# Squares of the MLP norms taken tile by tile behind the projections, and the decode step traced later, in a two-layer hybrid decoder step

## The chip, the core and the metric

The kernel runs on one core of a Trainium2 chip. The core has a matrix engine (PE in the profile), a vector engine (DVE), a scalar engine (ACT), a general engine (POOL), a queue engine that mostly issues DMAs (SP), and sixteen DMA engines. Each engine takes its instructions in the order in which they stand in its own queue, and waits there for what the next one needs. The metric is the device time of one execution in microseconds (us). Of the kernel before there are three timed runs, and one execution with a profile.

## The reference

One step of a decoder with two layers over 1,040 prompt positions (16 learned ones ahead of 1,024) and 8 decode tokens, with model width 1024 and MLP width 4096, all in fp32:

```python
for i in range(DEPTH):                       # layer 0: Conformer convolution; layer 1: RWKV-7
    hn = rmsnorm(h, norm_mix[i])
    out = conformer_conv(hn, ...) if i == 0 else rwkv7(hn, ...)
    h = h + out                              # out ends in a 1024x1024 projection (w_pw2, w_o)
    m = rmsnorm(h, norm_mlp[i])
    h = h + square(relu(m @ w_mlp_in[i])) @ w_mlp_out[i]
y = rmsnorm(h, norm_final)
# rmsnorm(x, g) = x * rsqrt(mean(x * x) + eps) * g
```

The decode tokens go through the same layers. In RWKV-7 each has a state of its own, 16 heads of 64x64, which is updated once (`S = S*w + sa*(kk*a) + v*k`, `y = S*r`); this is the "decode step" below. The prompt's RWKV-7 part runs in chunks of 64 positions.

## The kernel before

Activations lie transposed: 128 features on the partitions, eight tiles (k or m = 0 to 7) for the width of 1024, and up to 352 positions along the free axis. The positions are cut in three groups, g = 0, 1, 2. Every product is exact to fp32 by a split in a high and a low part: for each 128x128 block of weights PE does three matmuls (`mm3`, L187 to L189). ACT makes the high part of each weight (L157) and POOL subtracts to get the low part (L162, in pieces of 256 columns); activations are split by ACT (`hh`, `m_h`, `z_h`) and DVE (`hl`, `m_l`, `z_l`).

Layer 0 runs `post(0)`, `post(1)`, `post(2)` one after the other, about 300 us each. Each does the projection `pw2` (eight `ps_o` products, each added to `h` by DVE at L562), the norm of the MLP (`mlp_in`), and then the MLP: for j = 0 to 31 a product `ps_in` (24 matmuls), on which DVE applies relu and the norm's factor (`r`, L306), ACT squares (`s`) and splits; two steps later the products `out`, added to `h` by DVE at L319. Beside the MLP other work is handed out by `filler` at its points: the norm `norm_out(g-1)` of the group before, which makes the input of layer 1, the convolution of the next group and its layer norm. Behind `post(2)` comes `norm_out(2)` and the RWKV part. Layer 1 then runs `mixer_out(0)` (the projection `ps_oo` out of RWKV, added to `h` by DVE at L1459), the MLP of group 0, `mixer_out(1)`, `mixer_out(2)`, the MLP of groups 1 and 2 together, and the final norm. The recurrence of the last chunks (`until`), the decode step and the norms of the RWKV output (`norm_gates`, transposes on PE and work of DVE on `ey`, `eq`, `ez`) are handed out along `mixer_out(0)` and that first MLP.

A mean of squares in the kernel before is taken in one go, behind the last tile of `h`: ACT squares the eight tiles (L218), POOL adds the even ones up in one accumulator and DVE the odd ones in another (L223), and PE multiplies both by a constant matrix (`st_m`, `st_d`, L231), which sums over the partitions and spreads the mean over all of them. ACT takes the root, DVE the reciprocal (`rs`, L238). In `mlp_in` this stands behind the loop that makes `m_h` and `m_l` (L246, L247); the factor `rs` is used only at L306. In `norm_out` the factor is multiplied into `h` (L575).

The order on each engine is not the order of the code: a scheduler simulates the engines with a cost model and sets each queue's order from that, and the calls of `filler` set when a piece of side work becomes available to it.

## Time and profile before

| | us |
|---|---|
| median of three runs | 2909.58 (2907.05 to 2913.22) |
| profiled execution | 2902.45 |
| its span, first to last instruction | 2900.7 |
| PE busy in the span | 2682.1 (92%) |
| DVE, POOL, ACT busy | 1972.2 (68%), 1709.3 (59%), 1345.9 (46%) |
| mean granted clock of PE | 0.955 of full speed |

The profiled execution lies 7.1 us below the median of the runs, and 1.75 us of it lie outside the span. In the rows below, "[4.98 <-DVE h L319]" behind an instruction says that its engine had been idle for 4.98 us before it, and that the last thing it waited for was DVE's instruction on line 319 that writes `h`. Matmuls overlap, so their durations are longer than the distance from one to the next.

### The profile page before, as it was taken

The page shows a single profiled execution, that of the slowest core. Times are in us where ns is not written, and L with a number is a line of the kernel's source. Part 1 is how long each engine was busy: PE and PEld are TensorE (multiplying, and loading weights), DVE is VectorE, ACT ScalarE, POOL GpSimd, SP SyncE. Part 2 cuts the span into 40 slices and gives each one's busy share as a digit, 9 for nine tenths or more (in the row PEclk, how much of TensorE's full clock was granted, in tenths as well). Part 3 has the DMA queues.
Part 4 walks back from the last instruction along what each step waited for, and adds up shares of the span by engine and source line. Part 5 has one row for each costly group of instructions (what it writes and reads, how often), then busy time and mean ns, then how long its engine had stood idle before and what let it go on. Part 6 is the DMA issues. An engine that isn't in the chain of part 4 may idle for free.

```text
span 2900.7 us, 54435 instructions
## 1 busy us (share of the span) xinstructions
PE 2682.1 (92%) x20522; PEld 2561.1 (88%) x20522; DVE 1972.2 (68%) x3807; ACT 1345.9 (46%) x2511; POOL 1709.3 (59%) x2298
## 2 busy tenths in 40 slices
PE   8999899999998998877899889969999989999998
PEld 7999899989997998867788688858889989999998
DVE  5999999994476446367978786679856654443444
ACT  5545444543454334464666665634355542222223
POOL 6677778877787775445434453565548773433432
PEclk9999999999999999888899899989999999999999
DMA  6663444454445442676787787685567642222211
GB/s 180 171 184 93 139 133 138 144 157 138 139 145 164 139 139 86 197 196 168 212 206 207 204 214 181 174 209 152 134 169 224 183 135 85 66 69 70 66 59 41
DMA packets 659285, 428.34 MB, mean 148 GB/s; under 512 B 126840, under 2 KB 609208, under 8 KB 659022
## 3 DMA queue, kind: packets, MB, share of 16 engines
q1 hardware_dynamic: 652780, 421.93, 51.8%
q10 hardware_dynamic: 6018, 2.89, 0.4%
q8 instruction: 162, 2.65, 0.4%
q14 instruction: 101, 0.83, 0.1%
q0 software_dynamic: 224, 0.03, 0.0%
HBM read 353.03 MB, written 72.66 MB: 147 GB/s over the span
## 4 chain that ended last, share of the span: by engine, by line
PE 34%; DVE 6%; POOL 4%; DMA 3%; issue 2%; ACT 2%; SPq 0%; DVEq 0%; ACTq 0%; POOLq 0%
PE out L187 3%; PE ps_in L187 3%; PE ps_in L188 3%; PE out L188 3%; PE ps_in L189 3%; PE out L189 3%; POOL wo_lo L162 2%; PE A L1178 2%; POOL wi_lo L162 2%; DVE tt L1137 1%; PE ps_oo L187 1%; PE ps_oo L188 1%; PE ps_oo L189 1%; PE p_k L188 1%; PE p_k L187 1%
## 5 line engine op out<-in xcount | busy, mean ns | idle before, releaser
L162 POOL TENSOR_TENSOR wo_lo<-wo_raw,wo_hi 128x256 fp32r<-128x256 f32 x736 | 557.2, 789 | 309.7 <-ACT wo_hi L157 274.9
L162 POOL TENSOR_TENSOR wi_lo<-wi_raw,wi_hi 128x256 fp32r<-128x256 f32 x640 | 493.2, 802 | 274.3 <-ACT wi_hi L157 272.7
L187 PE MATMUL out<-hh,wo_hi 128*128 128x352 f32 (+2 forms) x1536 | 504.8, 329 | 31.2 <-ACT hh L140 15.5
L319 DVE TENSOR_TENSOR h<-h,out 128x352 f32<-128x352 f32 (+2 forms) x768 | 385.7, 510 | 194.2 <-PE out L189 193.6
L187 PE MATMUL ps_in<-m_h,wi_hi 128*128 128x352 f32 (+2 forms) x1536 | 497.8, 324 | 11.1 <-ACT m_h L246 10.5
L188 PE MATMUL out<-hh,wo_lo 128*128 128x352 f32 (+2 forms) x1536 | 498.9, 325 | 0.0
L189 PE MATMUL ps_in<-m_l,wi_hi 128*128 128x352 f32 (+2 forms) x1536 | 495.4, 323 | 2.7 <-DVE m_l L247 2.7
L188 PE MATMUL ps_in<-m_h,wi_lo 128*128 128x352 f32 (+2 forms) x1536 | 497.0, 324 | 0.0
L189 PE MATMUL out<-hl,wo_hi 128*128 128x352 f32 (+2 forms) x1536 | 491.9, 324 | 2.9 <-DVE hl L141 2.9
L483 DVE SCALAR_TENSOR_TENSOR cv<-u,wdw,cv 128x352 f32<-128x352 f32 (+2 forms) x720 | 378.0, 576 | 0.8
L157 ACT CAST wi_hi<-wi_raw 128x1024 fp32r<-128x1024 f32 x160 | 168.0, 1050 | 406.1 <-PE out L189 205.0
L157 ACT CAST wo_hi<-wo_raw 128x1024 fp32r<-128x1024 f32 x184 | 192.8, 1049 | 331.8 <-PE out L189 152.4
L187 PEld LDWEIGHTS out<-hh,wo_hi 128*128 128x128 f32 x1536 | 293.6, 191 | 39.7 <-DVE h L319 18.9
L187 PEld LDWEIGHTS ps_in<-m_h,wi_hi 128*128 128x128 f32 x1536 | 291.0, 189 | 13.2 <-ACT m_h L246 10.6
L189 PEld LDWEIGHTS out<-hl,wo_hi 128*128 128x128 f32 x1536 | 290.3, 190 | 4.8 <-DVE hl L141 4.3
L188 PEld LDWEIGHTS out<-hh,wo_lo 128*128 128x128 f32 x1536 | 293.4, 191 | 1.3
L189 PEld LDWEIGHTS ps_in<-m_l,wi_hi 128*128 128x128 f32 x1536 | 290.0, 189 | 4.6 <-DVE m_l L247 3.6
L188 PEld LDWEIGHTS ps_in<-m_h,wi_lo 128*128 128x128 f32 x1536 | 290.4, 189 | 1.6 <-issue 0.3
L306 DVE SCALAR_TENSOR_TENSOR r<-ps_in,rs_m 128x352 f32<-128x352 f32 (+2 forms) x192 | 98.5, 516 | 240.4 <-PE ps_in L189 233.2
L141 DVE TENSOR_TENSOR hl<-s,hh 128x352 fp32r<-128x352 f32 (+2 forms) x192 | 138.5, 723 | 102.6 <-ACT hh L140 102.4
L308 ACT ACTIVATE s<-r 128x352 f32<-128x352 f32 (+2 forms) x192 | 93.4, 490 | 134.8 <-DVE r L306 132.5
L1178 PE MATMUL A<-xa,bk 128*128 128x256 f32 x272 | 79.7, 412 | 16.9 <-DMA bk<-d_ab 12.2
(388 smaller groups left out, 6197.8 us busy)
## 6 DMA issues: line engine op xcount, KB each, us to landing
wi_raw<-in_w_mlp_in_dram SPq DMA_DIRECT2D x160, 512.0 KB, 4.1
wo_raw<-in_w_mlp_out_dram SPq DMA_DIRECT2D x160, 512.0 KB, 3.8
wr_raw<-in_rwkv_w_r_dram SPq DMA_DIRECT2D x32, 512.0 KB, 4.6
wk_raw<-in_rwkv_w_k_dram SPq DMA_DIRECT2D x32, 512.0 KB, 4.4
wv_raw<-in_rwkv_w_v_dram SPq DMA_DIRECT2D x32, 512.0 KB, 5.7
d_ab<-ab SPq DMA_DIRECT2D x32, 512.0 KB, 5.1
pg_raw<-in_conv_w_pw_dram SPq DMA_DIRECT2D x24, 512.0 KB, 4.9
pa_raw<-in_conv_w_pw_dram SPq DMA_DIRECT2D x24, 512.0 KB, 5.6
```

The costliest lines, as they stand in the source:

```text
L141: eng_lo.tensor_sub(lo, src, hi.bitcast(F32))
L157: nc.scalar.copy(hi[:, :a * b], raw[:, :a * b])
L162: eng_lo.tensor_sub(lo[:, cs], raw[:, cs], hi[:, cs].bitcast(F32))
L187: nc.tensor.matmul(ps, w[0], act[0], start=first, stop=False)
L188: nc.tensor.matmul(ps, w[1], act[0], start=False, stop=False)
L189: nc.tensor.matmul(ps, w[0], act[1], start=False, stop=last)
L306: nc.vector.scalar_tensor_tensor(r[:, :n], ps[:, :n], 0.0, rs[:, :n], op0=ALU.max, op1=ALU.mult)
L308: nc.scalar.activation(s[:, :n], r[:, :n], AF.Square)
L319: nc.vector.tensor_add(hv[:, 4 * i + m, :], hv[:, 4 * i + m, :], ps[:, :n])
L483: nc.vector.scalar_tensor_tensor(acc[m][:, :n], ug[:, m, j:j + n], wdw[:, m, j:j + 1], acc[m][:, :n], op0=ALU.mult, op1=ALU.add)
L1137: nc.vector.tensor_mul(o, ni[:, :j, j:j + 1].broadcast_to([B, j, wd]), ni[:, j:j + 1, j + 1:].broadcast_to([B, j, wd]))
L1178: nc.tensor.matmul(ps[:, i * 2 * P:(i + 1) * 2 * P], bk[:, j + i, :], xa[:, j + i].rearrange("p q x -> p (q x)"), start=True, stop=True)
```

## The change

The squares of a norm are now issued one by one, each behind the instruction that finishes its tile of `h`. `square_sums` gives a function `add(k, src)`, which squares tile k on ACT; the first tiles of each engine are held, the middle ones are added by the engines in turn, and the last two squares go to PE as they are. A mean so has up to four matmul inputs instead of two (accumulators and the squares of tiles 6 and 7). For the MLP norms POOL and DVE take turns; for `norm_out(0)` and `norm_out(1)` POOL alone adds, with three inputs for PE. In layer 0 the squares lie in `u[g]`, the convolution's input, which nobody reads any more by then (for `norm_out(2)` in temporary tiles); in layer 1 in three temporary buffers of their own (`sq`). The mean and `rs` of an MLP norm are now traced ahead of the loop for `m_h` and `m_l`. In layer 1 the side stream changes its order: the norms of the RWKV output of group 1 come first, then the decode step.

```diff
             for i, acc in enumerate(accs):
-                nc.tensor.matmul(ps[:, :n], ones_d, acc[:, :n], start=i == 0, stop=i == 1)
+                nc.tensor.matmul(ps[:, :n], ones_d, acc[:, :n], start=i == 0, stop=i == len(accs) - 1)
             return ps
+        def square_sums(n, name, place, engs, tag="acc"):
+            out, first = [], []
+            def add(k, src):
+                sq = place(k)
+                nc.scalar.activation(sq, src, AF.Square)
+                i = k % len(engs)
+                if k >= KT - 2:
+                    out.append(sq)
+                elif k < len(engs):
+                    first.append(sq)
+                else:
+                    if k < 2 * len(engs):
+                        out.append(stat(f"acc_{name}{i}", f"{tag}{i}", 1))
+                        a, b = out[i][:, :n], first[i]
+                    else:
+                        a = b = out[i][:, :n]
+                    engs[i].tensor_add(a, b, sq)
+            return add, out
...
-        def mlp_in(pl, hv, n, layer, name):
+        def mlp_in(pl, hv, n, layer, name, sums):
+            rs = rstd_of(mean_bcast(sums, n, name), n, 0, name, "rsm", 2)
             ah, al = new_act(pl, name, cur["wide"])
...
-            with tc.high_priority(offset=HP):
-                rs = rstd_of(mean_bcast(mean_parts(hv, n, name, True), n, name), n, 0, name, "rsm", 2)
             return ah, al, rs
...
-            def pw2(g, act):
+            def pw2(g, act, add):
...
                     nc.vector.scalar_tensor_tensor(h[g][:, m, :n], ps[:, :n], vec("b_pw2", m), h[g][:, m, :n],
                                                    op0=ALU.add, op1=ALU.add)
+                    add(m, h[g][:, m, :n])
...
             def norm_out(g):
...
-                parts = mean_parts(hv, n, f"d{g}", True)
-                yield MW
+                if g < 2:
+                    add, parts = square_sums(n, f"d{g}", lambda k: u[g][:, k, :n], (nc.gpsimd,), "accd")
+                else:
+                    add, parts = square_sums(n, f"d{g}", lambda k: tt(f"sqd{k}", "t1")[:, :n], (nc.gpsimd, nc.vector), "accm")
+                for k in range(KT):
+                    add(k, hv[:, k, :])
+                    yield MW / KT
...
-                pw2(g, ln_act[g])
+                add, sums = square_sums(n, f"m0{g}", lambda k: u[g][:, k, :n], (nc.gpsimd, nc.vector), "accm")
+                pw2(g, ln_act[g], add)
...
-            def mixer_out(g, residp, actp, fill):
+            def mixer_out(g, residp, actp, fill, add):
...
                     nc.vector.tensor_add(h1[:, m, :n], h1[:, m, :n], ps[:, :n])
+                    add(m, h1[:, m, :n])
...
+            def sums_of(g):
+                n = G2[g][1]
+                return square_sums(n, f"m1{g}", lambda k: cur["tmp"].tile([P, cur["n"]], F32, name=f"sq{g}_{k}", tag="sq", bufs=3)[:, :n],
+                                   (nc.gpsimd, nc.vector))
...
-                                ([decode_step(), norm_gates(GN_OF[1]), ng2], NGA))
-            mixer_out(0, residp, actp, fill)
+                                ([norm_gates(GN_OF[1]), decode_step(), ng2], NGA))
+            add, sums = sums_of(0)
+            mixer_out(0, residp, actp, fill, add)
```

Lines shift by 21 to 28 in the changed file: L306 becomes L327, L319 L340, L562 L583, L1459 L1487.

DVE where `post(2)` passes from its projection into its MLP, before: `ps_o2_7` is the last product of the projection, `acc_m02` belongs to the MLP's norm, `acc_d1` to `norm_out(1)`.

```order
L223 TENSOR_TENSOR acc_m021_9770<-acc_m021_9770,sq_m023_9772 128x348
L223 TENSOR_TENSOR acc_m021_9770<-acc_m021_9770,sq_m025_9775 128x348
L562 SCALAR_TENSOR_TENSOR h0_2_9459<-ps_o2_7_9715,pvec_85,h0_2_9459 128x348
L247 SCALAR_TENSOR_TENSOR m02_l_9742<-h0_2_9459,pvec_85,m02_h_9741 128x348
L223 TENSOR_TENSOR acc_m021_9770<-acc_m021_9770,sq_m027_9778 128x348
L238 RECIPROCAL rs_m02_9786<-sd_m02_9784 128x348
L223 TENSOR_TENSOR acc_d11_9824<-acc_d11_9824,sq_d13_9826 128x348
L223 TENSOR_TENSOR acc_d11_9824<-acc_d11_9824,sq_d15_9829 128x348
L223 TENSOR_TENSOR acc_d11_9824<-acc_d11_9824,sq_d17_9832 128x348
L306 SCALAR_TENSOR_TENSOR r0_0_2_9847<-ps_in0_0_2_9799,rs_m02_9786 128x348
```

The same place after the change:

```order
L583 SCALAR_TENSOR_TENSOR h0_2_9440<-ps_o2_5_9636,pvec_85,h0_2_9440 128x348
L270 SCALAR_TENSOR_TENSOR m02_l_9746<-h0_2_9440,pvec_85,m02_h_9745 128x348
L253 TENSOR_TENSOR acc_m021_9588<-acc_m021_9588,u2_125 128x348
L270 SCALAR_TENSOR_TENSOR m02_l_9746<-h0_2_9440,pvec_85,m02_h_9745 128x348
L583 SCALAR_TENSOR_TENSOR h0_2_9440<-ps_o2_6_9673,pvec_85,h0_2_9440 128x348
L270 SCALAR_TENSOR_TENSOR m02_l_9746<-h0_2_9440,pvec_85,m02_h_9745 128x348
L583 SCALAR_TENSOR_TENSOR h0_2_9440<-ps_o2_7_9709,pvec_85,h0_2_9440 128x348
L270 SCALAR_TENSOR_TENSOR m02_l_9746<-h0_2_9440,pvec_85,m02_h_9745 128x348
L260 RECIPROCAL rs_m02_9743<-sd_m02_9741 128x348
L327 SCALAR_TENSOR_TENSOR r0_0_2_9801<-ps_in0_0_2_9774,rs_m02_9743 128x348
L327 SCALAR_TENSOR_TENSOR r0_1_2_9841<-ps_in0_1_2_9816,rs_m02_9743 128x348
```

The three adds of `acc_d1` are gone from between `rs_m02` and the first `r`; those of `acc_m02` stand between the adds of the projection.

DVE at the end of `mixer_out(0)` before, from its last product but one to its last (`Sdec`, `t4`, `sa` belong to the decode step, `tt13`, `ni13` to the inverse for a chunk):

```order
L1358 TENSOR_REDUCE sa_23283<-t43_23737 128x4
L1359 TENSOR_TENSOR Sdec3_23736<-Sdec3_23736,dq_23071 128x256
L1137 TENSOR_TENSOR tt13_12_24174<-ni13_23884 128x228
L1360 TENSOR_TENSOR t43_23737<-sa_23283,dq_23071 128x256
L223 TENSOR_TENSOR acc_m101_23340<-acc_m101_23340,sq_m103_23342 128x328
L1138 TENSOR_TENSOR ni13_23884<-ni13_23884,tt13_12_24174 128x12x19
L1361 TENSOR_TENSOR Sdec3_23736<-Sdec3_23736,t43_23737 128x256
L1137 TENSOR_TENSOR tt13_11_24198<-ni13_23884 128x220
L1362 TENSOR_TENSOR t43_23737<-dq_23071 128x256
L223 TENSOR_TENSOR acc_m101_23340<-acc_m101_23340,sq_m105_23345 128x328
L1138 TENSOR_TENSOR ni13_23884<-ni13_23884,tt13_11_24198 128x11x20
L1459 TENSOR_TENSOR h1_0_22622<-h1_0_22622,ps_oo0_7_23270 128x328
```

After the change, around the same two adds (`sv`, `xa`, `nr` belong to the recurrence, `ey`, `ems` to the norms of the RWKV output):

```order
L1213 TENSOR_TENSOR xa1_12572<-A116_23171,m_ar_12477 64x2x64
L1214 TENSOR_TENSOR nr11_22923<-A116_23171,m_ar_12477 128x2x64
L1487 TENSOR_TENSOR h1_0_22592<-h1_0_22592,ps_oo0_6_23197 128x328
L1487 TENSOR_TENSOR h1_0_22592<-h1_0_22592,ps_oo0_7_23287 128x328
L270 SCALAR_TENSOR_TENSOR m10_l_23330<-h1_0_22592,pvec_85,m10_h_23329 128x328 x6
L1410 TENSOR_REDUCE ems4_0_23467<-ey4_0_23315 128x8
L270 SCALAR_TENSOR_TENSOR m10_l_23330<-h1_0_22592,pvec_85,m10_h_23329 128x328
L1411 SCALAR_TENSOR_TENSOR ey4_0_23315<-ems4_0_23467,ey4_0_23315 128x512
```

The decode step has left this stretch, and the adds of the squares have moved up ahead of it.

DVE in the MLP of group 0 of layer 1, from the factor of step j = 8 on, before:

```order
L306 SCALAR_TENSOR_TENSOR r1_8_0_24864<-ps_in1_8_0_24799,rs_m10_23356 128x328
L1364 TENSOR_TENSOR t414_24893<-Sdec14_24892,dq_23071 128x256
L1365 TENSOR_REDUCE yd_23284<-t414_24893 128x4
L1357 TENSOR_TENSOR t415_25013<-Sdec15_25012,dq_23071 128x256
L141 TENSOR_TENSOR hl10_8_24798<-s1_8_0_24866,hh10_8_24797 128x328
L1358 TENSOR_REDUCE sa_23283<-t415_25013 128x4
L1287 TENSOR_TENSOR fs13_24751<-S13_24697,wc_12552 128x512
L1359 TENSOR_TENSOR Sdec15_25012<-Sdec15_25012,dq_23071 128x256
L1360 TENSOR_TENSOR t415_25013<-sa_23283,dq_23071 128x256
L1185 TENSOR_TENSOR xa0_12601<-A144_24755,m_ar_12507 64x2x64
L1186 TENSOR_TENSOR nr14_24570<-A144_24755,m_ar_12507 128x2x64
```

The same place after:

```order
L327 SCALAR_TENSOR_TENSOR r1_8_0_24818<-ps_in1_8_0_24753,rs_m10_23327 128x328
L1385 TENSOR_TENSOR t40_24958<-Sdec0_24957,dq_24824 128x256
L141 TENSOR_TENSOR hl10_8_24752<-s1_8_0_24820,hh10_8_24751 128x328
L1386 TENSOR_REDUCE sa_24955<-t40_24958 128x4
L1387 TENSOR_TENSOR Sdec0_24957<-Sdec0_24957,dq_24824 128x256
L1315 TENSOR_TENSOR fs13_24712<-S13_24658,wc_12522 128x512
L1388 TENSOR_TENSOR t40_24958<-sa_24955,dq_24824 128x256
L1213 TENSOR_TENSOR xa0_12571<-A144_24716,m_ar_12477 64x2x64
L1214 TENSOR_TENSOR nr14_24545<-A144_24716,m_ar_12477 128x2x64
L1389 TENSOR_TENSOR Sdec0_24957<-Sdec0_24957,t40_24958 128x256
L1213 TENSOR_TENSOR xa0_12571<-A144_24716,m_ar_12477 64x2x64
```

Before, the decode step is in its last pieces (`Sdec14`, `Sdec15`) here; after, it begins (`Sdec0`), and 134 of its 144 DVE instructions stand between the steps j = 8 and j = 15, where the 30 instructions of the gates that stood there are gone.

## Rows read from the trace of the kernel before

**Rows 1.** Page, part 1: engine busy us (share of the span) xinstructions.
```profile
PE 2682.1 (92%) x20522; PEld 2561.1 (88%) x20522; DVE 1972.2 (68%) x3807; ACT 1345.9 (46%) x2511; POOL 1709.3 (59%) x2298
```

**Rows 2.** PE timeline: start, us, instruction [idle before it <-releaser]; seven longest related waits.
```profile
608.88 0.66 PE L187 MATMUL out<-hh,wo_hi 128*128 128x348 f32 x1 [4.98 <-DVE h L319]
...
901.92 0.66 PE L187 MATMUL out<-hh,wo_hi 128*128 128x348 f32 x1 [13.13 <-ACT hh L140]
...
1162.67 0.59 PE L187 MATMUL p_g<-hxh,g_hi 128*128 128x272 f32 x1 [8.15 <-ACT hxh L140]
...
1959.07 0.64 PE L187 MATMUL ps_in<-m_h,wi_hi 128*128 128x328 f32 x1 [10.46 <-ACT m_h L246]
...
2339.80 0.86 PE L231 MATMUL st_m<-acc_m,ones_d 128*128 128x352 f32 x2 [1.95 <-POOL acc_m L223]
2343.33 0.66 PE L187 MATMUL ps_oo<-z_h,wo_hi 128*128 128x352 f32 x1 [2.67 <-ACT z_h L140]
...
2384.40 0.43 PE L189 MATMUL ps_in<-m_l,wi_hi 128*128 128x352 f32 x1 [2.43 <-DVE m_l L247]
```

**Rows 3.** Same view, DVE, in the wait that ends at 901.9.
```profile
890.74 7.02 DVE L223 TENSOR_TENSOR acc_d<-acc_d,sq_d 128x348 f32<-128x348 f32 x1 [3.17 <-ACT sq_d L218]
898.31 0.52 DVE L223 TENSOR_TENSOR acc_d<-acc_d,sq_d 128x348 f32<-128x348 f32 x1 [0.56 <-ACT sq_d L218]
899.39 0.52 DVE L223 TENSOR_TENSOR acc_d<-acc_d,sq_d 128x348 f32<-128x348 f32 x1 [0.56 <-ACT sq_d L218]
```

**Rows 4.** Same view, POOL, in the same wait.
```profile
890.14 2.76 POOL L162 TENSOR_TENSOR wi_lo<-wi_raw,wi_hi 128x256 fp32r<-128x256 f32 x4
...
893.74 2.75 POOL L162 TENSOR_TENSOR wo_lo<-wo_raw,wo_hi 128x256 fp32r<-128x256 f32 x4
896.47 0.91 POOL L223 TENSOR_TENSOR acc_d<-acc_d,sq_d 128x348 f32<-128x348 f32 x1
```

**Rows 5.** Windows: stretch, length, busy (instructions) by engine, PE clock, DMA share, GB/s.
```profile
902.00:905.50 3.50, 3.50 (x13) 3.50 (x14) 1.86 (x5) 1.78 (x5) 0.00 (x0) 0.52 0.00 0
```

**Rows 6.** DVE timeline at the second group of the layer-1 MLP.
```profile
2375.84 7.54 DVE L223 TENSOR_TENSOR acc_m<-acc_m,sq_m 128x352 f32<-128x352 f32 x2 [1.48 <-ACT sq_m L218]
```

**Rows 7.** DVE timeline ahead of the wait that ends at 1162.67.
```profile
1154.09 5.22 DVE L575 SCALAR_TENSOR_TENSOR h<-h,pvec,rs_d 128x348 f32<-128x348 f32 x8
```

**Rows 8.** DVE timeline in the wait that ends at 1959.07.
```profile
1955.42 1.05 DVE L1359 TENSOR_TENSOR Sdec<-Sdec,dq 128x256 f32<-128x256 f32 x1
...
1957.23 0.41 DVE L1360 TENSOR_TENSOR t<-sa,dq 128x256 f32<-128x256 f32 x1
...
1959.95 0.48 DVE L1459 TENSOR_TENSOR h<-h,ps_oo 128x328 f32<-128x328 f32 x1
```

**Rows 9.** Windows of layer 1: output projection, then four blocks of column steps j.
```profile
1885.00:1959.00 74.00, 49.09 (x501) 43.43 (x487) 52.59 (x114) 28.15 (x56) 44.39 (x56) 0.85 0.81 207
1959.00:2007.00 48.00, 45.89 (x418) 38.87 (x420) 44.58 (x105) 22.56 (x46) 24.48 (x30) 0.88 0.58 149
2007.00:2067.00 60.00, 59.03 (x492) 48.74 (x484) 52.85 (x120) 21.50 (x41) 32.44 (x40) 0.91 0.52 139
2067.00:2122.00 55.00, 55.00 (x659) 48.75 (x659) 39.82 (x93) 28.43 (x60) 27.94 (x35) 1.00 0.65 157
2122.00:2175.00 53.00, 51.85 (x609) 45.93 (x608) 32.41 (x66) 27.42 (x57) 26.74 (x33) 1.00 0.57 162
```

**Rows 10.** Lines, DVE, whole span: decode operations, dearest and cheapest of nine.
```profile
L1362 DVE TENSOR_TENSOR t<-dq 128x256 f32<-128x256 f32 x16 | 10.3, 644 | 0.1
...
L1358 DVE TENSOR_REDUCE sa<-t 128x4 f32<-128x256 f32 x16 | 6.5, 406 | 0.1
```

**Rows 11.** Lines, DVE, 2067 to 2175: the dearest of seven gate lines.
```profile
L1383 DVE SCALAR_TENSOR_TENSOR ey<-ems,ey 128x512 f32<-128x512 f32 (+1 forms) x5 | 4.4, 875 | 0.1
```

**Rows 12.** PE timeline around the matmuls of one mean.
```profile
882.07 1.33 PE L231 MATMUL st_m<-acc_m,ones_d 128*128 128x348 f32 x4
882.97 0.59 PE L189 MATMUL ps_in<-m_l,wi_hi 128*128 128x348 f32 x1
```

More of the change, by code (lines that the diff above doesn't have):

```diff
@@ L584, in post @@
                     nc.sync.dma_start(h[g][:, :, :n], d_x2)
-                pw2(g, ln_act[g])
+                add, sums = square_sums(n, f"m0{g}", lambda k: u[g][:, k, :n], (nc.gpsimd, nc.vector), "accm")
+                pw2(g, ln_act[g], add)
                 hv = h[g][:, :, :n]
-                ah, al, rs = mlp_in(actp[1], hv, n, 0, f"m0{g}")
+                ah, al, rs = mlp_in(actp[1], hv, n, 0, f"m0{g}", sums)
                 gens, cnt = [], 0
@@ L1511, in until, with group @@
                     yield wait
-            def group(g, actp, hidp):
+            def sums_of(g):
+                n = G2[g][1]
+                return square_sums(n, f"m1{g}", lambda k: cur["tmp"].tile([P, cur["n"]], F32, name=f"sq{g}_{k}", tag="sq", bufs=3)[:, :n],
+                                   (nc.gpsimd, nc.vector))
+            def group(g, actp, hidp, sums):
                 n = G2[g][1]
                 hv = hl[g][:, :, :n]
-                return (g, hv, n, *mlp_in(actp, hv, n, 1, f"m1{g}"), hidp)
+                return (g, hv, n, *mlp_in(actp, hv, n, 1, f"m1{g}", sums), hidp)
             ng2 = norm_gates(GN_OF[2])
@@ L1521, in hybrid_step @@
                                 ([until(NCH - 1)], FA * CHUNK_WAIT * (NCH - 1 - st["done"])),
-                                ([decode_step(), norm_gates(GN_OF[1]), ng2], NGA))
-            mixer_out(0, residp, actp, fill)
-            mlp(1, [group(0, actp, hidp)], 2, nc.gpsimd, nc.vector, fill)
+                                ([norm_gates(GN_OF[1]), decode_step(), ng2], NGA))
+            add, sums = sums_of(0)
+            mixer_out(0, residp, actp, fill, add)
+            mlp(1, [group(0, actp, hidp, sums)], 2, nc.gpsimd, nc.vector, fill)
             for _ in rest:
@@ L1532, in hybrid_step @@
             fill, rest = filler(2 * KT, ([ng2], NGB))
-            mixer_out(1, residp2, actp, fill)
+            add, sums = sums_of(1)
+            mixer_out(1, residp2, actp, fill, add)
             for _ in rest:
@@ L1537, in hybrid_step @@
                 nc.scalar.dma_start(o_conv_sample[0, q, 0:CB - 1, :], state_conv[0, q, 1:CB, :])
-            g1 = group(1, actp, hidp)
+            g1 = group(1, actp, hidp, sums)
             fill, rest = filler(2 * KT + MLP2_POINTS, ([ranked(FN, final(0))], FB))
-            mixer_out(2, residp2, actp2, fill)
+            add, sums = sums_of(2)
+            mixer_out(2, residp2, actp2, fill, add)
             end = []
@@ L1547, in fill2 @@
                 (end[0][0] if end else fill)()
-            mlp(1, [g1, group(2, actp2, hidp2)], 1, nc.gpsimd, nc.vector, fill2, done)
+            mlp(1, [g1, group(2, actp2, hidp2, sums)], 1, nc.gpsimd, nc.vector, fill2, done)
             for it in (rest, end[0][1], final(2)):
```

## The prediction

> **What bounds the kernel now.** I read the page first: PE is busy for 2682.1 of 2900.7 us [rows 1]. So a change on the other engines can only pay in the 219 us in which PE stands still, or in which it runs at the lower clock. Next I read the timeline of PE for its waits and kept those that end on work this change touches [rows 2]: 4.98 us in the MLP of `post(1)` (it waits for DVE's adds to `h`, which stand behind the second norm of that stretch), 13.13 us at the start of `post(2)`, 8.15 us behind `norm_out(2)`, 10.46 us between `mixer_out(0)` and the MLP of layer 1, 1.95 and 2.67 us between `mixer_out(1)` and `mixer_out(2)`, and 2.43 us at the start of the last MLP. They add up to 43.8 us. Third, the timelines of DVE and POOL inside these waits, to see what was late. Last, the windows of the stretch in which the decode step runs, since its move loads DVE elsewhere.
>
> The largest wait shows the pattern. The DVE add of `acc_d` at 890.74 takes 7.02 us; its two fellows take 0.52 [rows 3]. All that time POOL works without a pause, with subtractions for the weights and its own adds [rows 4]. So a DVE add with both inputs in SBUF does not get its turn while POOL runs back to back. The first `r`, which PE needs by way of `hh`, stands behind the three adds. At the last MLP two such adds take 7.54 us together [rows 6]. The Trainium skill, "SBUF — State Buffer", section "Who interferes with whom", names this pair as the one that contends and says that whichever starts first holds the port for its whole instruction. By that the add would have waited for one POOL instruction (0.91 at most here) and taken some 1.4 us; the row shows a wait over nine of them. By the page's rule the add would have ended 5.4 us sooner, and the sum below would be 6 us smaller (rival 3).
>
> **The change, part by part.** All sums are against the profiled execution; I carry the difference over to the median, which lies 7.1 us above it.
>
> A, `norm_out(1)` leaves DVE. The three adds are gone from before the first `r`; POOL alone adds, and the mean moves to about j = 14 of that MLP, where nobody waits for it. The wait of 13.13 goes. Behind it PE ran at 0.52 of its clock, nearly all at the lower of its two levels (1.2 GHz), for 3.5 us [rows 5], which costs half of that, 1.7. At most -14.8; if DVE's adds for the MLP norm a little earlier are held up in their turn, only the two short adds and the gaps before them go, some -2. What is late next is `hh` itself (factor, square, split: three instructions of some 0.5 us), so a us or two of wait remains. POOL has two more adds in its queue for each of the first two groups, 0.91 each [rows 4], ahead of the splits of weights; it is idle for 41% of the span [rows 1], so I cost them at 0. I take -12.
>
> B, the start of the last MLP: the adds move up between the adds of `mixer_out(2)`, out of the way of `m_l`. The wait of 2.43 goes and with it about 1.7 of low clock as at A: -4.1 to 0. I take -3.
>
> C, between `mixer_out(1)` and `mixer_out(2)`: PE waits 1.95 for POOL's last add and 2.67 behind `m_h` on ACT. Now the last two squares go to PE without an add. But ACT's order there stays crowded: -4.6 to +1. I take -3.
>
> D, the wait of 4.98 in `post(1)`: three DVE adds fewer ahead of `h`, but the reciprocal and eight products of the same norm stay. -5 to 0; I take -3.
>
> E, `norm_out(2)`: PE now has the four matmuls of the mean right behind the last `out`, ahead of `p_r`, so this is a new wait: PE stands there, and `p_r` behind it, until the eight squares and the adds are done. Eight such elementwise passes in one run took 5.22 us [rows 7], which I take as the bound of that. In return the chain to the normed `h` is shorter: its eight products began at 1154.09 and ended at 1159.31, and `p_g` could start only at 1162.67, 8.15 late. With the mean ready before `p_r` starts, that wait can go whole. -8.15 to +5; nearer to the measured wait, I take -5.
>
> F, the end of `mixer_out(0)`: before the last add to `h` (1959.95) DVE works on the decode step, an operation taking 1.05 us beside POOL and 0.41 without [rows 8]. The decode step leaves this stretch, the mean's adds move up. The wait is 10.46; the clock averages 0.85 and 0.88 in the windows on either side [rows 9], and of that at most 4 us belong to this wait. What is late next is the split of `m_l` behind the last add, about 3 us, and the loading of `z`, which is not touched. -14 to 0; I take -7.
>
> G, the decode step in the MLP of layer 1. It has 144 DVE instructions in nine lines of 16; the nine sum to 76.4 us, the dearest 10.3 and the cheapest 6.5 [rows 10], 0.53 on the mean. In the two blocks of 2067 to 2175 DVE is busy for 39.82 and 32.41 of 108 us [rows 9], 35.8 idle. Sixteen decode instructions stand there now, 134 will: 118 more, or 62.5 us at 0.53; the gates' 28 instructions leave, seven lines whose dearest is 4.4 us [rows 11], 18.8 together. The balance, +43.7, is 7.9 more than DVE's idle time. At 0.41 each it would be +29.6 and fit; at 1.0 (beside POOL) +99.2, or 63 over. Against that, the blocks of 1959 to 2067 lose their 83 decode instructions. PE recorded 3.1 us of idle time there, and at clocks of 0.88 and 0.91 of full speed the loss is up to 5.8 and 5.4 us; 4 of it I have counted under F. So the gain there is at most 10. G lies between -10 and +63. I take 0, about where +8 and -10 leave it, as the mean of 0.53 is what these very operations took. On SP's queue the step's 16 loads and 16 stores move with it, away from the loads of `z` and of weights in `mixer_out(0)` to a stretch where only weights are loaded; that too is in F and G, at 0.
>
> H, matmuls. There are sixteen more inputs to the means (two more in each of six MLP norms, one each in `norm_out(0)` and `norm_out(1)`, two in `norm_out(2)`). A mean with two inputs took from 882.07 to 882.97 [rows 12], 0.45 each: 16 x 0.45 = +7.2. PE is the bound, so most of this counts; where it waits anyhow (E, F) it is free. 0 to +8; I take +7.
>
> Squares stay eight to a mean. The smaller shifts of order in the RWKV part I cost at 0, with 10 us either way.
>
> Sum: -12 - 3 - 3 - 3 - 5 - 7 + 0 + 7 = -26. The profiled execution would take 2876.5; the median 2883.6, so 2884.
>
> **Rivals.**
>
> 1. The decode step makes DVE the bound of j = 8 to 15 (slower). For: all decode operations now stand in two blocks with little room, and PE waits for DVE's `h` within a few of its banks. Against: their mean so far, in stretches as crowded, fits nearly. It decides where the overflow passes 26 + the relief of up to 10, so 36; that is a balance of 72, or (72 + 18.8) / 118 = 0.77 us for each decode operation. At 1.0 it would be 63 - 10 - 26 = +27, 2937. Between them I put it at 2920.
>
> 2. The hold-up of DVE adds moves with them (no change). The MLP norms' adds now stand among the adds of the projections, where POOL splits the weights of that very projection; an add of 7 us there makes `h` late for the product that needs its bank. For: twelve DVE adds remain in the MLP norms, two in each, and each has two inputs in SBUF. Against: PE has several products in hand there, and of the adds in the first 300 us and in `post(1)` none left a wait among the rows. Three such adds in the open would cost 3 x 7 = 21: -26 + 21 = -5, 2905, which can't be told from no change.
>
> 3. A DVE add waits for one POOL instruction at most, and the 7.02 us have another cause, which stays (a smaller gain). For: elsewhere an operation beside POOL loses about one POOL instruction, 1.05 against 0.41 [rows 8]. Against: the long add ends at 897.76, right behind POOL's run (897.38). A then loses 5.4 to 6 of its 12: -20, 2890. This is how the page cited above reads.
>
> 4. Everything at its better end (A -14, F -12, G -10, E -8): -26 - 2 - 5 - 10 - 3 = -46, 2864.
>
> **How the numbers follow.** The forecast has 0.5, rival 1 0.15, rival 2 0.13, rival 3 0.10, rival 4 0.12. What can be told from no change in this kernel is about 0.2%, 5.8 us. Faster by more: forecast, rivals 3 and 4 and a quarter of rival 2, 0.75; same 0.10; slower 0.15. The range leaves out the better half of rival 4 and the worse half of rival 1: 2864 to 2912.
>
> **What would show it.** A: no `acc_d` add on DVE at the start of `post(2)`, and the wait there under 3 us. F: the wait for `m_h` at the first `ps_in` of layer 1 under 5 us, and that `ps_in` earlier by about 7 relative to the start of `mixer_out(0)`. E: `p_g` some 5 us sooner after the last `out`. G: the four blocks of 1959 to 2175, 216 us now, as long as before; if they take over 230, rival 1 holds, and decode operations show a mean of 0.77 or more. H: PE's matmuls of line 231 cost 7 us more. Rival 2 shows as a DVE add of over 3 us with a wait of PE behind it among `ps_o` or `ps_oo`. The prediction fails if any one block gets longer by more than 20 us.

## The result: slower, 2924.5 us

| | before | after |
|---|---|---|
| median, us | 2909.01 (2907.05 to 2913.22, 5 runs) | 2924.54 (2919.09 to 2927.12, 5 runs) |
| ratio to before, 95% interval | | 1.0049 (1.0034 to 1.0065) |
| profiled execution, us | 2902.45 | 2919.09 |

The forecast was 2884, with a range up to 2912. The change is slower by 0.5%, clear of noise. The page of the profile after has PE busier by 34.7 us than before [rows 1], with sixteen matmuls more to do, which the profile shows as 32 passes:

```profile
PE 2716.8 (93%) x20554; PEld 2578.6 (88%) x20554; DVE 1974.6 (68%) x3794; ACT 1348.5 (46%) x2515; POOL 1698.8 (58%) x2295
```

The profiled execution is longer by 16.6 us, so PE even waits less than before; all of the added time counts as work of PE. Where it lies is worked out from PE's timelines, by the start of the first or last matmul of a name:

| stretch | before | after | difference |
|---|---|---|---|
| start to the last `out` of `post(2)` | 1135.7 | 1121.1 | -14.6 |
| from there to the last `p_v` (end of RWKV's projections) | 745.8 | 742.5 | -3.3 |
| to the first `ps_in` of layer 1 (`mixer_out(0)`) | 77.6 | 99.1 | +21.5 |
| MLP of group 0, j = 0 to 7 | 108.2 | 120.0 | +11.8 |
| the same, j = 8 to 15 | 107.9 | 119.2 | +11.3 |
| the same, j = 16 to the first `ps_oo` of group 1 | 131.5 | 134.4 | +2.9 |
| from there to the end | 594.0 | 581.0 | -13.0 |

The change gains 31 us at both ends and loses 47.5 between `mixer_out(0)` and the end of the next MLP. The waits of PE that answer to those of [rows 2], in the timeline of the changed kernel:

```profile
983.06 0.63 PE L187 MATMUL out<-hh,wo_hi 128*128 128x348 f32 x1 [7.40 <-DVE r L327]
...
1128.06 2.69 PE L231 MATMUL st_d<-acc_d,ones_d 128*128 128x348 f32 x4 [6.59 <-POOL acc_d L253]
...
1149.25 0.59 PE L187 MATMUL p_r<-mh,wr_hi 128*128 128x272 f32 x1 [16.48 <-ACT mh L140]
...
1874.81 0.64 PE L187 MATMUL ps_oo<-z_h,wo_hi 128*128 128x328 f32 x1 [4.84 <-ACT z_h L140]
...
1881.00 0.64 PE L189 MATMUL ps_oo<-z_l,wo_hi 128*128 128x328 f32 x1 [3.64 <-DVE z_l L141]
...
1896.48 0.64 PE L187 MATMUL ps_oo<-z_h,wo_hi 128*128 128x328 f32 x1 [8.46 <-ACT z_h L140]
...
1962.74 0.42 PE L187 MATMUL ps_in<-m_h,wi_hi 128*128 128x328 f32 x1
```

Gone are the waits of 4.98, 13.13, 8.15, 10.46 (the first `ps_in` waits for nothing), 2.67 and 2.43; of 1.95 there is 1.18 left. New are 7.40 us at j = 14 of `post(2)`, 6.59 and 16.48 us at the entry of RWKV, and 4.84, 3.64 and 8.46 us for `z` in `mixer_out(0)`. Even so PE stands still for less time in `mixer_out(0)` than before (by the first of the windows below, 96 - 78.61 = 17.4 us, against 74 - 49.09 = 24.9 [rows 9]), and yet it takes 21.5 us more. In the MLP behind it PE shows hardly a wait. Its waits between 1960 and 2083 (total, times, longest), in full:

```profile
PE gg L1242 <- ACT no L1212: 0.4, 1, 0.4
```

0.4 us in 123. And yet j = 0 to 7 takes 11.8 us more than before, with DVE relieved. The windows of the projection and of the two pairs of blocks (as in [rows 9]: stretch, length, busy time and instructions of PE, PEld, DVE, ACT and POOL, PE's clock, DMA share, GB/s):

```profile
1867.00:1963.00 96.00, 78.61 (x469) 60.32 (x470) 58.87 (x122) 32.48 (x63) 40.17 (x54) 0.77 0.60 162
1963.00:2083.00 120.00, 119.56 (x910) 93.90 (x910) 61.50 (x124) 50.77 (x108) 52.85 (x66) 0.89 0.53 132
2083.00:2202.00 119.00, 110.19 (x1291) 96.03 (x1291) 109.05 (x246) 48.25 (x96) 59.95 (x72) 0.98 0.55 144
```

In the middle row PE is "busy" for 119.56 of 120 us at a clock of 0.89, while DVE has fallen to 61.50, from 97.4 in the 108 us before [rows 9]. But the clock is no difference here: before it was 0.88 and 0.91 in the two blocks [rows 9]. (In `mixer_out(0)` it is one: 0.77 against 0.85.) The timeline of PE shows what it does there:

```profile
2069.46 0.31 PE L1242 MATMUL po<-p,gg 32*32 32x32 f32 x6
2069.70 0.41 PE L187 MATMUL out<-hh,wo_hi 128*128 128x328 f32 x1
2070.04 0.24 PE L1242 MATMUL po<-p,gg 32*32 32x32 f32 x2
2070.22 0.41 PE L188 MATMUL out<-hh,wo_lo 128*128 128x328 f32 x1
2070.56 0.24 PE L1242 MATMUL po<-p,gg 32*32 32x32 f32 x2
2070.73 0.43 PE L189 MATMUL out<-hl,wo_hi 128*128 128x328 f32 x1
```

Large ones in a row, in the kernel before:

```profile
1909.65 0.31 PE L189 MATMUL ps_oo<-z_l,wo_hi 128*128 128x328 f32 x1
1909.80 0.31 PE L187 MATMUL ps_oo<-z_h,wo_hi 128*128 128x328 f32 x1
```

Two small matmuls of the recurrence (`po`, 32x32) stand between any two large ones. From one large matmul to the next it takes 0.52 us (2069.70, 2070.22, 2070.73), where large ones in a row follow each other by 0.15 (1909.65 to 1909.80). A matmul's record there stays 0.41 long, so none of this is a gap. What I had not looked for in the order is this: the number of places at which PE goes from other matmuls back to the large ones of `mm3`, from `mixer_out(0)` to j = 15, is 97 before and 189 after (below called returns).

### The profile page after: what moved, and what is told of

Its sections match the earlier page's. It is cut to its first block, busy times and chain, and to the rows that moved or that the text cites. A ratio compares the mean times of both kernels' runs of the same rounds, so it can differ in the third digit from the quotient of the medians.

```text
span 2917.4 us, 54478 instructions
## 1 busy us (share of the span) xinstructions
PE 2716.8 (93%) x20554; PEld 2578.6 (88%) x20554; DVE 1974.6 (68%) x3794; ACT 1348.5 (46%) x2515; POOL 1698.8 (58%) x2295
## 4 chain that ended last, share of the span: by engine, by line
PE 66%; DVE 13%; POOL 6%; DMA 5%; issue 4%; ACT 3%; SPq 0%; DVEq 0%; POOLq 0%; ACTq 0%
PE ps_in L189 7%; PE ps_in L187 7%; PE ps_in L188 7%; PE out L187 7%; PE out L189 7%; PE out L188 7%; POOL wo_lo L162 4%; POOL wi_lo L162 2%; DVE cv L504 2%; PE A L1206 2%; PE ps_o L189 1%; PE ps_o L188 1%; PE ps_o L187 1%; DVE mx L814 1%; PE ps_oo L187 1%
## 5 line engine op out<-in xcount | busy, mean ns | idle before, releaser
L162 POOL TENSOR_TENSOR wi_lo<-wi_raw,wi_hi 128x256 fp32r<-128x256 f32 x640 | 486.5, 792 | 308.2 <-ACT wi_hi L157 292.3
L340 DVE TENSOR_TENSOR h<-h,out 128x352 f32<-128x352 f32 (+2 forms) x768 | 385.3, 510 | 199.3 <-PE out L189 198.8
L187 PEld LDWEIGHTS out<-hh,wo_hi 128*128 128x128 f32 x1536 | 291.8, 190 | 28.1 <-DVE h L340 14.0
L327 DVE SCALAR_TENSOR_TENSOR r<-ps_in,rs_m 128x352 f32<-128x352 f32 (+2 forms) x192 | 98.6, 515 | 228.2 <-PE ps_in L189 224.5
L141 DVE TENSOR_TENSOR hl<-s,hh 128x352 fp32r<-128x352 f32 (+2 forms) x192 | 150.2, 783 | 102.4 <-ACT hh L140 102.3
L162 POOL TENSOR_TENSOR wv_lo<-wv_raw,wv_hi 128x256 fp32r<-128x256 f32 x96 | 80.3, 866 | 28.9 <-ACT wv_hi L157 28.8
```

The source lines that it names most:

```text
L141: eng_lo.tensor_sub(lo, src, hi.bitcast(F32))
L162: eng_lo.tensor_sub(lo[:, cs], raw[:, cs], hi[:, cs].bitcast(F32))
L187: nc.tensor.matmul(ps, w[0], act[0], start=first, stop=False)
L327: nc.vector.scalar_tensor_tensor(r[:, :n], ps[:, :n], 0.0, rs[:, :n], op0=ALU.max, op1=ALU.mult)
L340: nc.vector.tensor_add(hv[:, 4 * i + m, :], hv[:, 4 * i + m, :], ps[:, :n])
```

## The experiments

All times are medians; "before" ran beside them, at 2907 to 2913. Behind a time stands its ratio to that, with the 95% interval. The returns are counted in each built kernel's order on PE, in `mixer_out(0)` and in j = 0 to 3, 4 to 7, 8 to 11, 12 to 15; the three stretches are those of the table above.

| kernel | returns | `mixer_out(0)` | j 0-7 | j 8-15 | median |
|---|---|---|---|---|---|
| before | 10, 16, 42, 11, 18 | 77.6 | 108.2 | 107.9 | 2909.0 |
| the change | 61, 56, 49, 14, 9 | 99.1 | 120.0 | 119.2 | 2924.5 |
| e_dec | 8, 31, 36, 27, 23 | 79.0 | 102.1 | 122.8 | 2886.0 |
| b_dec | 56, 27, 48, 14, 9 | 101.3 | 106.2 | 117.6 | 2945.8 |
| a_nodec | 61, 56, 48, 13, 9 | 99.5 | 117.2 | 111.2 | 2914.1 |
| b_nodec | 22, 56, 61, 10, 10 | 72.2 | 124.4 | 109.9 | 2925.3 |
| e_re | 14, 5, 20, 13, 5 | 82.2 | 88.2 | 105.0 | 2878.2 |
| e_accre | 6, 7, 18, 10, 4 | 82.3 | 87.9 | 106.4 | 2847.6 |
| e_accdecre | 22, 6, 8, 11, 6 | 86.5 | 87.0 | 94.8 | 2839.8 |
| b_re | 59, 6, 8, 12, 7 | 93.6 | 96.9 | 89.6 | 2913.6 |

**Which part costs.** Two kernels with one line changed each: the change with the decode step traced first again (e_dec), and the kernel before with nothing but the decode step traced later (b_dec).

```diff
-                                ([norm_gates(GN_OF[1]), decode_step(), ng2], NGA))
+                                ([decode_step(), norm_gates(GN_OF[1]), ng2], NGA))
```

> The change with the decode step traced first again, as before. Theory (the move of the decode step alone costs: with its DVE work gone from there, the recurrence's small matmuls are ordered one by one between the matmuls of the output projection and of the MLP, and every such switch holds PE up; later DVE is the bound): the stretch from the last p_v to the first ps_in of layer 1 is back near 77 us (99 with the whole change), the MLP of group 0 near 348 us (374), and the total some 47 us under the whole change, 2878 (2870 to 2890). Rival (the squares' new buffers in layer 1, 4,224 bytes, make the loads of h and z late): both stretches stay within 5 us of the whole change, total 2915 to 2925.

> The kernel before with nothing changed but the decode step traced behind the gates of group 1. Theory (the move alone costs): 20 to 47 us slower than before, 2930 to 2956, with 131 instead of 68 switches from the recurrence's matmuls back to the projection's and the MLP's up to step j = 7. Rival (the cost comes from the squares in layer 1): within 6 us of before.

e_dec took 2886.0 (ratio to before 0.9935, 0.9917 to 0.9953), b_dec 2945.8 (1.0129, 1.0112 to 1.0146). The move of the decode step costs 38.5 us with the squares and 38.6 without (33 and 38 by the ratios), and both totals lie in the ranges expected; the rest of the change gains 23 (21 against the runs of before beside it). The rival of e_dec, the squares' new buffers in layer 1, is out: e_dec keeps them. In e_dec the MLP of group 0 came back only to 355.6, not 348: j = 8 to 15 stayed long, with 50 returns there instead of 29 and a clock of 0.93 instead of 1.00.

**Load or order?** The same two kernels without the decode step's arithmetic on DVE, so that DVE has some 76 us less to do [rows 10].

```diff
                     nc.sync.dma_start(S, s_in[:, vs, :])
-                    nc.vector.tensor_mul(t4, S, overv(2))
-                    nc.vector.tensor_reduce(sa[:, vs], t4, axis=AX.X, op=ALU.add)
...
-                    nc.vector.tensor_reduce(yd[:, vs], t4, axis=AX.X, op=ALU.add)
+                    if hv == 0:
+                        nc.vector.tensor_mul(yd, dq[:, 0], dq[:, 4])
                     nc.sync.dma_start(s_out[:, vs, :], S)
```

> The whole change without the arithmetic of the decode step on DVE (143 of 144 operations left out; its loads, stores and transposes stay). PE's order keeps 61, 56 and 48 returns to large matmuls in the output projection and in j = 0 to 3 and 4 to 7. Theory (order up to j = 7, DVE's load only from j = 8 on): from the last p_v to the first ps_in 95 to 103 us and j = 0 to 7 115 to 124, as with the whole change; j = 8 to 15 falls from 119 to 98 to 108; total 2905 to 2915. Rival (DVE's load is all of it): the three stretches go to 77, 105 and 95 us, total 2870 to 2885.

> The kernel before without the arithmetic of the decode step on DVE. The scheduler's order then has 22, 56 and 61 returns to large matmuls in the output projection and in j = 0 to 3 and 4 to 7 (10, 16 and 42 before). Theory (taking DVE work away splinters PE's order): j = 0 to 7 gets longer than the 108 us of before, although 83 DVE operations have gone from it, and the total is no better than 2900. Rival (DVE bounds that stretch): j = 0 to 7 under 95 us, total 2880 to 2890.

Work taken away made the kernel before slower: b_nodec 2925.3 (1.0044, 1.0029 to 1.0059). The window of its j = 0 to 7:

```profile
1960.00:2084.00 124.00, 121.92 (x862) 94.54 (x861) 54.01 (x111) 44.14 (x85) 50.84 (x67) 0.87 0.46 115
```

DVE is busy for 54.01 of 124 us, and the stretch is 16 us longer than with the decode step in it (108.2). a_nodec came to 2914.1, inside what was expected, but its j = 8 to 15 is 111.2, above the 98 to 108 that I had put down: DVE's load there explains 8 us, not all of it. With the order kept (187 returns instead of 189) the load is worth 10 us of the total.

**The price of a return, by itself.** 512 small matmuls whose result is not used were added to the kernel before, in its last MLP, where no recurrence runs: once two behind every three large ones (p_each), once in as few places as the scheduler let them have (p_run).

```diff
+                        if probe:                              # p_each
+                            tiny(dm, m * 4 + j * 2)
+                            tiny(dm, m * 4 + j * 2 + 1)
...
+                        if probe and m == 3 and j == 1:        # p_run
+                            for q in range(16):
+                                tiny(dm, q)
```

> The kernel before with 512 small matmuls (32x32, result unused) added to the last MLP, two after each group of three matmuls, in 255 places of PE's order. Theory (each return from small matmuls to the large ones holds PE up by some 0.3 us): 255 x 0.3 = 77 us over before. Rival (a small matmul costs its own 0.04 us wherever it stands): 512 x 0.04 = 20 us over before, as much as with the same matmuls in few places.

> The same 512 small matmuls, in 82 places of PE's order instead of 255. Theory: 173 returns fewer, so some 52 us under the kernel with 255 places. Rival: the same time as that within 6 us.

They took 3019.3 (1.0371, 1.0337 to 1.0404) and 2964.0 (1.0181, 1.0158 to 1.0204). The 173 returns more cost 55.2 us, 0.32 each (0.28 to 0.36: there are two runs of each, and those of p_each, 3013.0 and 3025.5, lie 12 us apart); what p_run costs over before, 53.6, leaves (53.6 - 82 x 0.32) / 512 = 0.05 for a small matmul itself. So p_each lies 109 us over before, more than either expectation for it: both prices count. PE's timeline in p_each (`dm` are the added ones; each shows as two passes):

```profile
2520.12 0.31 PE L312 MATMUL dm<-ident 32*32 32x32 f32 x4
2520.35 0.43 PE L187 MATMUL out<-hh,wo_hi 128*128 128x352 f32 x1
2520.62 0.32 PE L188 MATMUL out<-hh,wo_lo 128*128 128x352 f32 x1
2520.78 0.32 PE L189 MATMUL out<-hl,wo_hi 128*128 128x352 f32 x1
2521.03 0.31 PE L312 MATMUL dm<-ident 32*32 32x32 f32 x4
```

Three large and two small matmuls take 0.91 us (2520.12 to 2521.03); without returns it would be 3 x 0.16 + 2 x 0.05. PE shows no idle time here either. One view does tell of it: the waits of PEld, the weight loads (total, times, longest), first in p_each and then in p_run ("issue" stands for a wait for nothing that the profile shows):

```profile
PEld dm L312 <- issue: 54.8, 251, 0.2
```

```profile
PEld dm L312 <- issue: 17.5, 80, 0.2
```

PEld is idle for 0.2 us at 251 and at 80 places, in front of the first small load behind a large one. That is the larger part of the 0.32, and its count is nearly that of the returns (255 and 82).

Not every return has this price. In the changed kernel two `A` matmuls, which are 128x128 like the large ones, stand between two of these:

```profile
2047.56 0.31 PE L189 MATMUL out<-hl,wo_hi 128*128 128x328 f32 x1
2047.71 0.59 PE L1206 MATMUL A<-xa,bk 128*128 128x256 f32 x2
2047.95 0.50 PE L187 MATMUL ps_in<-m_h,wi_hi 128*128 128x328 f32 x1
```

They add 0.24 us, which is about what their 512 columns take at the pace of the large ones (328 in 0.15). With two matmuls of 128x64 (`W`) in between, large ones stand 0.6 us apart:

```profile
2065.84 0.42 PE L187 MATMUL out<-hh,wo_hi 128*128 128x328 f32 x1
2066.19 0.33 PE L1272 MATMUL W<-sv,xa 128*64 128x64 f32 x2
2066.45 0.41 PE L188 MATMUL out<-hh,wo_lo 128*128 128x328 f32 x1
```

The returns of the table count all of these places alike, so 0.32 for each of them is an estimate.

**The change with its order kept together.** One number: the recurrence of the last chunks gets a higher rank with the scheduler. The decode step stays late.

```diff
-        RE = 0
+        RE = 300
```

> The whole change with one number altered: the last chunks' recurrence in layer 1 gets a higher rank with the scheduler (300 instead of 0). The decode step stays late. PE's order has 14, 5 and 20 returns from small to large matmuls in the output projection and in j = 0 to 3 and 4 to 7, instead of 61, 56 and 49; 57 up to j = 15 instead of 189. Theory (the returns are the cost, not the decode step's place): 132 x 0.32 = 42 us less, 2882 (2872 to 2892); j = 8 to 15 stays long, about 115, since DVE is full there. Rival (the late decode step costs by its load on DVE): over 2908.

2878.2 (0.9879, 0.9853 to 0.9906), 46 us under the change, where 132 returns fewer at 0.32 give 42. The three stretches themselves got 63 us shorter and RWKV 20 longer (762.1 from the last `out` to the last `p_v`, against 742.5), so the two totals agree better than the stretches do. PE's timeline and the windows of j = 0 to 7 and 8 to 15 in this kernel:

```profile
2033.81 1.15 PE L1272 MATMUL W<-sv,xa 128*64 128x64 f32 x32
2034.89 0.69 PE L1242 MATMUL po<-p,gg 32*32 32x32 f32 x32
2035.51 0.42 PE L188 MATMUL out<-hh,wo_lo 128*128 128x328 f32 x1
```

```profile
1966.00:2054.00 88.00, 86.21 (x983) 78.64 (x984) 62.27 (x131) 52.73 (x112) 54.47 (x68) 1.00 0.68 165
2054.00:2159.00 105.00, 97.34 (x1129) 87.72 (x1126) 93.38 (x211) 44.52 (x85) 55.05 (x67) 0.98 0.60 158
```

All 32 `po` now run in 0.62 us; in the changed kernel they were strewn over 10 us (2069.46 to 2079.2). The clock is 1.00 in j = 0 to 7, where it was 0.89: with the splintered order PE was also at the lower of its levels, 1.2 GHz, for part of the time. That the small matmuls between the large ones bring the clock down does not follow. In p_each two stand behind every three large ones, and the clock stays at 1.00:

```profile
2550.00:2650.00 100.00, 100.00 (x712) 83.33 (x711) 30.41 (x54) 20.02 (x32) 27.45 (x38) 1.00 0.18 54
```

The same number in the kernel before (b_re):

> The kernel before with the recurrence ranked up, nothing else. The returns do not get fewer as a whole (59, 6, 8, 12 and 7 against 10, 16, 42, 11 and 18; 92 against 97). Theory (the rank helps only by the number of returns): 2900 to 2915. Rival (the rank itself makes the recurrence's chain shorter): 2885 or less.

2913.6 (1.0001, 0.9990 to 1.0011): the rank by itself brings nothing. But it moved time: the three stretches got 14 us shorter and RWKV longer, which the number of returns in layer 1 alone does not tell.

**The entry of RWKV.** In the changed kernel the three accumulators `accm0`, `accm1`, `accd0` are new tiles. Buffers are laid out one above the other, and `h` of group 2 stands above them: in the built kernels it lies at bytes 151,744 to 163,008 of each partition before and 155,968 to 167,232 after. The first `mx` buffer of the RWKV part lies at 165,664 to 166,752 in both. So `mx` now has to wait until the normed `h` is stored. DVE after:

```profile
1133.39 2.33 DVE L260 RECIPROCAL rs_d<-sd_d 128x348 f32<-128x348 f32 x1 [9.49 <-ACT sd_d L258]
1135.75 6.55 DVE L602 SCALAR_TENSOR_TENSOR h<-h,pvec,rs_d 128x348 f32<-128x348 f32 x8
1148.24 1.33 DVE L814 SCALAR_TENSOR_TENSOR mx<-xx,pvec,hx 128x272 f32<-128x272 f32 x3 [5.94 <-DMA d_hn<-h]
```

The wait of 5.94 us "<-DMA d_hn<-h" is that store. Before, `mx` ran ahead of the products:

```profile
1136.81 1.32 DVE L786 SCALAR_TENSOR_TENSOR mx<-xx,pvec,hx 128x272 f32<-128x272 f32 x3
```

e_acc puts the accumulators above the weights instead.

```diff
             open_weights(l0, 0, {"w": 5}, 0)
+            cur["accp"] = pool(l0, "accp0", 1)
...
-                        out.append(stat(f"acc_{name}{i}", f"{tag}{i}", 1))
+                        pl = cur["accp"] or cur["stat"]
+                        out.append(pl.tile([P, cur["n"]], F32, name=f"acc_{name}{i}", tag=f"{tag}{i}", bufs=1))
```

> The whole change, with the three new accumulators of layer 0 in a pool behind the weights instead of ahead of the tile of h. Theory (their 4,224 bytes push h of group 2 into the memory of the first mx buffers, so RWKV's first mixed inputs wait for the store of the normed h): p_r starts within 4 us of the last out (28 us with the whole change) and the start of p_v of the first group comes 5 to 9 us sooner; total 2916 (2912 to 2921). Rival (the wait is only that of the mean's four matmuls ahead of p_r): p_r still over 15 us behind the last out, total unchanged within 3 us.

```profile
1121.84 0.39 PE L188 MATMUL p_r<-mh,wr_hi 128*128 128x272 f32 x1 [1.82 <-ACT mh L141]
```

```profile
1120.79 2.00 DVE L817 SCALAR_TENSOR_TENSOR mx<-xx,pvec,hx 128x272 f32<-128x272 f32 x3
...
1133.98 6.55 DVE L605 SCALAR_TENSOR_TENSOR h<-h,pvec,rs_d 128x348 f32<-128x348 f32 x8
```

`p_r` starts 2.1 us behind the last `out` (28.1 with the change), `mx` ahead of the products. The median fell by 20 to 2904.7, more than expected; its profiled execution, 2911.9, lies 7 above its median, so the other stretches of that trace can't be added up to the 20. The pairs beside it say the same: e_accdec against e_dec -16, e_accre against e_re -31.

> The accumulators of layer 0 behind the weights, and the decode step traced first as before. 104 returns up to j = 7 and 15 (7, 15, 39, 27, 23 by block + rest). Theory: 2886 of the run with the decode step first, less 13 to 20 for the accumulators, 2869 (2862 to 2876). Rival (the gain at RWKV's entry is given back later): 2880 or more.

> The rank of the recurrence as in the run beside it, and the three accumulators of layer 0 behind the weights. Theory (two separate costs add up): 42 + 20 us under the whole change, 2863 (2855 to 2873). Rival (both remove the same lateness at the start of layer 1): no better than either alone, 2882 or more.

e_accdec took 2870.1 (0.9850, 0.9826 to 0.9873), as expected, e_accre 2847.6 (0.9771, 0.9743 to 0.9798), below its range of 2855 to 2873. The rival, that both remove the same lateness, is out; but together they bring 77 us, 11 more than the 46 and 20 that they bring alone, and where these come from is open.

**The squares in the dead inputs.** The memory of `u[0]` and `u[1]` is not idle in `post(2)`: the first tiles of the RWKV part (`hx`, `xx`) are laid over it, and `hx` is loaded at 966.49 instead of 829.71, behind `norm_out(1)`. e_t1 puts those squares in temporary tiles.

```diff
-                    add, parts = square_sums(n, f"d{g}", lambda k: u[g][:, k, :n], (nc.gpsimd,), "accd")
+                    add, parts = square_sums(n, f"d{g}", lambda k: tt(f"sqd{g}_{k}", "t1")[:, :n], (nc.gpsimd,), "accd")
```

> The whole change, with the squares of norm_out of groups 0 and 1 in temporary tiles instead of the convolution's inputs. Theory (the memory of those inputs was not free: the first tiles of the RWKV part lie in it, and are filled only when norm_out(1) has read its squares): xx comes back to the start of post(2) as before, the wait of 7.4 us at j = 14 of post(2) shrinks to under 3, total 2918 (2914 to 2922). Rival (that wait is due to norm_out(1)'s eight products alone): it stays over 5 us, total unchanged within 3 us.

```profile
985.85 0.40 PE L187 MATMUL out<-hh,wo_hi 128*128 128x348 f32 x1 [2.53 <-DVE r L327]
```

The wait shrank from 7.40 to 2.53, `hx` was loaded at 869.81, but the total did not change beyond noise (2921.8; 1.0053, 1.0037 to 1.0069): another wait, of 3.81 us for `hl`, came up before 884.53. With the other two edits it was no help at all:

> Accumulators behind the weights, the recurrence ranked up, and the squares of norm_out of groups 0 and 1 in temporary tiles. Theory (the wait at j = 14 of post(2) is 2.5 instead of 7.4 us, its clock loss with it): 4 to 6 us under the run without the temporary tiles. Rival (as measured with the whole change, where it gave nothing): the same within 3 us.

2858.4 (0.9808, 0.9786 to 0.9830), 11 us over e_accre. In the profiled executions the difference lies in RWKV (24 us more from the last `out` to the last `p_v`); why is open.

**Late or early, once the order is kept.** The fastest kernel, with the decode step first:

> The fastest kernel so far (accumulators behind the weights, recurrence ranked up) with the decode step traced first again. 53 returns to large matmuls up to j = 15 instead of 45. Theory (with PE's order kept together, the place of the decode step is worth little either way): 2848 to 2860. Rival (the late decode step still costs by filling DVE at j = 8 to 15): 2838 or less, j = 8 to 15 under 97 us.

2839.8 (0.9745, 0.9729 to 0.9762), the fastest of all. The windows of j = 8 to 15, with the decode step late (e_accre) and early (e_accdecre):

```profile
2015.00:2121.00 106.00, 97.65 (x1118) 87.74 (x1117) 93.30 (x210) 44.37 (x84) 57.67 (x70) 0.97 0.59 156
```

```profile
2029.00:2124.00 95.00, 92.53 (x1055) 84.97 (x1054) 71.00 (x154) 48.65 (x97) 54.73 (x67) 1.00 0.66 178
```

With it DVE is busy for 93.30 of 106 us, without for 71.00 of 95. So the late decode step does cost some 11 us there, of which j = 0 to 7 gives nothing back. Of these, 6 are waits of PE (106 - 97.65 = 8.4 us against 95 - 92.53 = 2.5), the rest is work of PE (63 passes more in the window). The total differs by 8, not much more than the runs of e_accre among themselves would allow (2840.3 to 2852.9). Both sides had a part of it: the stretch is as the rival said, the sum is between the two.

## Why the prediction was wrong

The steps that failed are G, "I take 0", and F, "I take -7". Both counted the decode step as so many operations of DVE that leave one stretch and load another, and its leaving as a relief. I weighed DVE's busy time and PE's waits, and never PE's order between these places, although the trace of before holds the pattern, from 2053 to 2058:

```profile
2053.32 0.24 PE L1214 MATMUL po<-p,gg 32*32 32x32 f32 x2
2053.50 0.41 PE L189 MATMUL out<-hl,wo_hi 128*128 128x328 f32 x1
2053.84 0.24 PE L1214 MATMUL po<-p,gg 32*32 32x32 f32 x2
```

Measured, the move costs 38.5 us where F and G together stood at -7. By the price above, the returns are the largest part of it but not the whole: the change has 64 more than e_dec, b_dec 57 more than before, which at 0.32 makes 20.5 and 18 us. DVE's load adds 8 to 12. What is left, 6 to 12 us, was not traced to a cause; the clock in `mixer_out(0)` (0.77 in the change, 0.90 in e_dec) may be part of it.

- The scheduler fills each queue by its own estimate of when work can start. With the decode step gone from DVE, the recurrence's small matmuls become ready one by one while PE is in the large ones, and it puts them in between. Shown: fewer DVE operations (b_nodec) give more returns and more time; a higher rank (e_re) gives fewer of both; the price of a return is 0.32 us by p_each and p_run. That the scheduler's estimate is the reason is argued from its way of working and from these orders; it was not measured by itself. Of the 46 us between the change and e_re, 42 would be returns at that price.
- DVE's load at j = 8 to 15 is the smaller part: 8 us of that stretch by a_nodec, 11.6 by the last pair. Rival 1 had the sign, and with 2920 nearly the time, but for the larger part by another mechanism; that its time came so near is luck. The four blocks took 239 us, over the 230 from which it was to hold; but decode operations took 79.6 us for 144, 0.55 each, far from the 0.77 that it needed.

The other terms, by the stretches of the first table:

- A (-12): the wait of 13.13 went as forecast, with the three adds. But `post(2)` from its first `ps_o` to its last `out` got only 1.5 us shorter; the wait of 7.40 came up instead. The price was put on what was removed, not on the memory that the squares now hold; but e_t1, which frees that memory, gained nothing in all.
- D (-3): 4.98 gone. `post(0)` and `post(1)` got 5.2 and 7.7 shorter together with the sixteen-matmul bill; better than forecast.
- E (-5): the new wait in front of `p_r` was in the sum with a bound of 5; it was 6.59 and 16.48. The bound came from the length of the squares, and the larger part was a buffer that stood in another buffer's way. RWKV gave it back in this trace (-3.3 in all); freed of it the kernel gains 16 to 31.
- B and C (-6): -13.0; two of the three waits are gone, the third is 1.18.
- F, apart from the decode step: the wait of 10.46 went, as forecast. But `mixer_out(0)` now waits 16.9 us for `z`, whose loading F had named as what would be late next, without a price.
- H (+7): not seen by itself; outside E, the matmuls of the changed means show one wait, the 1.18.

Without F and G the sum stood at -19, and the change without the move of the decode step measured -21 to -23: the squares behind the projections do gain. That the sum fits is in part luck, since its terms do not: A gave 1.5 for 12, B and C 13 for 6.

Rival 2, that the hold-up moves, came in part, and mostly not in the adds. DVE operations with two inputs in SBUF that lasted long in the changed kernel, and what POOL did meanwhile:

```profile
295.72 6.32 DVE L141 TENSOR_TENSOR hl<-s,hh 128x352 fp32r<-128x352 f32 x1
1874.84 6.92 DVE L141 TENSOR_TENSOR z_l<-zr,z_h 128x328 fp32r<-128x328 f32 x3 [4.39 <-ACT z_h L140]
2389.76 5.38 DVE L253 TENSOR_TENSOR acc_m<-sq,sq 128x352 f32<-128x352 f32 x1 [2.70 <-ACT sq L241]
```

```profile
1872.35 8.23 POOL L162 TENSOR_TENSOR wo_lo<-wo_raw,wo_hi 128x256 fp32r<-128x256 f32 x12
2389.16 5.60 POOL L162 TENSOR_TENSOR wi_lo<-wi_raw,wi_hi 128x256 fp32r<-128x256 f32 x8
```

The add at 2389.76 has no wait of PE behind it. The split `z_l` (the first of the three takes 6.1 us) makes the wait of 3.64 in `mixer_out(0)`, and the split `hl` at 295.72 one of 3.25 in `post(0)`. The add at 2389.76 also speaks against rival 3: it ends 0.4 us behind a run of eight instructions of POOL, as the add of 7.02 did behind its run, not behind the first of them. When a DVE operation is held for a whole run and when not was not measured; another add, at 2397.80, took 0.80 us in the middle of such a run.
